# Values and gates of layer 1: another order of buffers, tables formed at the beginning, one projection moved

## The chip, the cores and the metric

The kernel runs on one core of one Trainium2 chip. The metric is the device time of one execution in microseconds. Three runs of the kernel before took 3581.37 to 3582.74 us, their median is 3581.59 us. A core has five engines with instruction streams of their own, each executed in order: TensorE (PE, with its weight loads as PEld), VectorE (DVE), ScalarE (ACT), GpSimd (POOL) and SyncE (SP, which here only issues DMAs). DMAs are issued from SP, ACT and POOL and run on 16 DMA engines.

## The reference

The reference is a two-layer backbone on 2048 latent tokens (32 rows of 64) and 256 context tokens, width 1024, in float32. Layer 0 (attention and gated linear attention) is not touched. Layer 1 is this:

```
h, hc  = modulated rms_norm of x and of the context
q, k, v, z = split(h @ w_in, 4)                 # w_in: 1024 x 4096; 16 heads of 64
q, k   = rms_norm per head
s_lat  = q . k (window of 8 rows x 16 columns) * scale + bias[head]
s_ctx  = q . k_ctx * scale
p      = softmax(concat(s_lat, s_ctx))
o      = p @ v
x      = x + gate * ((o * silu(z)) @ w_out)
```

## The kernel before

Tokens are worked on in 18 tiles of 128: tiles 0 and 1 are the context, 2 to 17 the latent tokens. `w_in` of layer 1 is cut into eight column blocks of 512, `j` = 0 to 7: 0 and 1 are the queries, 2 and 3 the keys, 4 and 5 the values, 6 and 7 the gates `z`. A matrix product in float32 precision is made of three passes: each operand is split into a high part and a rest, and `hi*hi`, `lo*hi` and `hi*lo` are summed (L129 to L131 for one tile, L190 to L192 for a pair of tiles). One projection of one tile and one block, called a cell (t, j) here, is 24 matmuls of 512 columns; a cell of gates serves a pair of tiles and is 96 matmuls of 256 columns.

Layer 1 has three stages. `odd_qk` projects queries and keys, tile by tile, and ends with the gates' block 6 of tiles 16 and 17 and the values' block 4 of these two tiles. Its work buffers come from a pool `osA`: the gains, two squares, small sums, four `onat` (a projected tile on its way to memory), two each of `oqh` and `oql` (transposed keys and queries), and four `okt` of 8 KB per partition, the keys in another order of columns. Values go to memory by POOL's DMAs (`store_v`, L1420, two for each tile), gates by POOL's (`store_z`, L1425), keys by SP's (`K1`) and POOL's (`K1t`, L1386).

`odd_vz`, the stage of the change, does two things in one interleaved stream:

- the remaining projections of values and gates (`cell`): tiles 17 and 16 first, then pairs of tiles downward. Each pair of tiles needs its modulated rows again: `reload(1, t)` loads them as `x` from the scratch tensor H (SP, L376), ACT makes the high part `hhi`, DVE the rest `hlo` (L380), in two slots that alternate with the tile number. A slot is free after the last cell of the tile that holds it. Gates are formed by ACT (tanh) and DVE (L1407), values copied by ACT, all into `ovz`, of which there are three.
- for each of 16 heads and 2048 queries, the maximum of the scores (`maxes`), which the third stage needs to form the softmax. For each head a table of biases (`mtab`, 128 x 1798, two buffers) is loaded by SP (L1476), and POOL adds two masks to it (L1477, L1478); keys `mk` (L1474) are loaded for two heads at a time and queries `mq` (L1465) for 512 at a time; ACT puts the queries into a buffer `mz` in which the other head's half is zeroed (DVE memsets, L1459); TensorE forms scores of 128 queries against the context (L1492) and against their window (L1499) in six PSUM banks `mx`, DVE reduces them (L1494) and adds the bias and reduces in one instruction (L1505).

`weave` draws from both generators: 0.57 steps of the maxima for each step of the projections (a step is three matmuls of 512 columns, or six of 256), and a projection step is held behind the maximum that lies 15 steps back.

`odd_attention`, the third stage, is not touched.

What sets the order of the instructions: the program is written with tiles in pools; when it is built, a planner with a cost estimate plays the program through and fixes, for each engine, the order in which instructions are issued: the oldest in program order among those that are ready by its estimate. On the chip each engine then keeps this order and waits, whatever has become ready behind. `issue_after(i)` adds a pure ordering: what is traced inside is placed behind `i` on its engine. Buffers of a pool lie one behind another in the order in which their names are first used; a pool that is opened where an earlier one was closed lies in the same place, and a buffer there waits for the last use of each old buffer that it overlaps. So `osB` and `omB`, the pools of `odd_vz`, lie where `osA` was.

Of the kernel before, what the change touches and what calls it, by code (L numbers as in the profile page):

```python
# [10 lines left out]
F32 = mybir.dt.float32  # L11
F32R = mybir.dt.float32r
AF = mybir.ActivationFunctionType
ALU = mybir.AluOpType
# [3 lines left out]
P = 128  # L18
D = 1024
# [4 lines left out]
NT = T // P  # L24
# [64 lines left out]
class Kern:  # L89
# [279 lines left out]
        nc.scalar.dma_start(self.H[l, t], x[:])  # L369
        return hi, lo  # L370

    def reload(self, l, t):

        nc, sp = self.nc, self.prp
        x = self.tl(sp, [P, D], "x", bufs=1)
        nc.sync.dma_start(x[:], self.H[l, t])  # L376
        h = x[:].rearrange("p (k t) -> p k t", k=KD)
        hi, lo = self.slots(t)
        self.act(hi, h)
        nc.vector.tensor_tensor(out=lo, in0=h, in1=hi, op=ALU.subtract)  # L380
        return hi, lo
# [902 lines left out]
    def odd_qk(self, ws, win, hT):  # L1284
        nc = self.nc
# [6 lines left out]
        with ExitStack() as es:  # L1292
            sp = self.pool(es, "osA", bufs=2, side="left", reuse_waits="tile")
# [98 lines left out]
            done = lambda j: j in nxt and self.od_ahead(win, ws, nxt[j])  # L1392
            cells = self.cells(list(range(NT)), (2, 3, 0, 1), lambda t, j: j > 1 or t >= NCT)[:-8]
            for j in (0, 1, 2, 3, 6, 4):
                cells += [((NT - 2, NT - 1), j)] if j == 6 else [(t, j) for t in (NT - 2, NT - 1)]
# [31 lines left out]
    def odd_vz(self, ws, win, hT):  # L1427
        nc = self.nc
        self.M1 = self.scr("M1", (16, SEQ), F32)
        NR, NC = (len(b) for b in BLOCKS["q"])  # L1430
        with ExitStack() as es:
            sp = self.pool(es, "osB", bufs=2, side="left", reuse_waits="tile")
            mp = self.pool(es, "omB", bufs=2, side="left", reuse_waits="tile")
            pp = self.pool(es, "opB", bufs=2, space=PSUM, reuse_waits="tile")
            mk = self.tl(mp, [P, NR + NC], "maskq", bufs=1)
            nc.sync.dma_start(mk[:], self.i["maskq"])

            def cell(t, j):
                wh, wl = win[j]
                w = lambda k: wh[:, k, :], lambda k: wl[k][:]  # L1440
                if j > 5:
                    for b in (0, 2):
                        ps = self.tl(pp, [P, 512], "gm")
                        yield from self.pair_steps(ps, b, w)
                        n = self.tl(sp, [P, 512], "ovz", bufs=3)
                        self.gate(n, ps[:])
                        self.store_z(t, (j - 6) * 4 + b, n)
                    return
                hi, lo = hT[t]
                ps = self.tl(pp, [P, 512], "gm")  # L1450
                yield from self.mm3_steps(ps[:], (lambda k: hi[:, k, :], lambda k: lo[:, k, :]), w, range(KD))
                n = self.tl(sp, [P, 512], "ovz", bufs=3)
                self.act(n[:], ps[:])
                self.store_v(t, j - 4, n)

            zq = [[self.tl(mp, [P, 512], f"mz{i}{a}", F32R, bufs=1) for a in range(2)] for i in range(2)]
            for i in range(2):
                for z in zq[i]:
                    nc.vector.memset(z[64 - i * 64 : 128 - i * 64].bitcast(F32), 0.0)  # L1459

            def queries(n, eng):
                h, g = divmod(n, 4)
                b = (h % 2) * 64
                q = self.tl(mp, [P, 512], "mq", F32R, bufs=1)
                eng.dma_start(q[b : b + 64].bitcast(F32), self.Q1[0, h // 2, b : b + 64, g * 512 : g * 512 + 512])  # L1465
                return q

            def maxes():
                post, q = None, queries(0, nc.sync)
                for h in range(16):  # L1470
                    j, b = h // 2, (h % 2) * 64
                    if b == 0:
                        k = self.tl(mp, [P, T], "mk", F32R, bufs=2)
                        nc.sync.dma_start(k[:].bitcast(F32), self.K1[j])  # L1474
                    tb = self.tl(mp, [P, NR, NC], "mtab", bufs=2)
                    nc.sync.dma_start(tb[:], self.i["rpb_q"][h].rearrange("p (r c) -> p r c", r=NR))  # L1476
                    nc.gpsimd.tensor_tensor(out=tb[:], in0=tb[:], in1=mk[:, :NR].unsqueeze(2).to_broadcast([P, NR, NC]), op=ALU.add)  # L1477
                    nc.gpsimd.tensor_tensor(out=tb[:], in0=tb[:], in1=mk[:, NR:].unsqueeze(1).to_broadcast([P, NR, NC]), op=ALU.add)  # L1478
                    m = self.tl(mp, [P, 16, 5], "mm")
                    nc.vector.memset(m[:], -3e38)  # L1480
                    kl = k[:, CTX:].rearrange("d (r c) -> d r c", r=32)
                    for R in range(16):
                        g, c = divmod(R, 4)
                        if c == 0:
                            zt = zq[h % 2][g % 2]
# [6 lines left out]
                        nc.tensor.matmul(pc[:, c % 2, :], lh, k[:, :CTX], start=True, stop=True)  # L1492
                        if c % 2 == 1:
                            nc.vector.tensor_reduce(out=m[:, R - 1 : R + 1, 0], in_=pc[:], axis=AX.X, op=ALU.max)  # L1494
                        (r0, nr), (c0, w) = rect("q", g, c)
                        ps = self.tl(pp, [P, 512], "mx", bufs=6)
                        a, n, d = even(c0, w)
                        ps = ps[:, : nr * n].rearrange("p (r c) -> p r c", r=nr)
                        mm = nc.tensor.matmul(ps, lh, kl[:, r0 : r0 + nr, a : a + n], start=True, stop=True)  # L1499
                        ps = ps[:, :, d : d + w]  # L1500
                        n = 1
                        for ro, ri, rn in pieces("q", 0, g, r0, nr):
                            for co, ci, cn in pieces("q", 1, c, c0, w):
                                s = ps[:, ro : ro + rn, co : co + cn]
                                nc.vector.tensor_tensor_reduce(out=s, in0=s, in1=tb[:, ri : ri + rn, ci : ci + cn], scale=1.0,  # L1505
                                                               scalar=-3e38, op0=ALU.add, op1=ALU.max, accum_out=m[:, R, n : n + 1])
                                n += 1
                        if R == 4 and post:
                            post()
                        yield mm  # L1510
                    mc = self.tl(mp, [P, 16], "mc", bufs=1)
                    nc.vector.tensor_reduce(out=mc[:], in_=m[:], axis=AX.X, op=ALU.max)

                    def post(h=h, mc=mc):
                        pt = self.tl(pp, [P, 512], "mx", bufs=6)
                        nc.tensor.transpose(pt[:16, :P], mc[:], self.ident[:])
# [422 lines left out]
```

## Time and profile before

| what | value |
|---|---|
| median of three runs | 3581.59 us |
| the profiled execution | 3587.56 us |
| its span, first to last instruction | 3585.8 us |
| mean granted clock of TensorE in it | 0.988 |

`odd_vz` begins at about 2572 us of the span and its last projections end at about 3011 us. In the profile's rows a time stands in front (us from the span's start), then the duration, the engine, the line of the kernel, the operation, and `out<-in` by the program's names; in brackets the idle time of the engine just before and what ended it. `x2` behind a row means that two like instructions are merged. In a table of stretches, the busy time of each engine stands with the number of its instructions, then the granted clock of TensorE, the busy share of the DMA engines and their GB/s. In a list of waits stand the waiting engine, line and tile, what it waited for, and then us in total, times, and the longest. Where a DMA's time to landing is given, it is from issue until its semaphore came, as minimum, median and maximum.

### The profile page before, as it was taken

The numbers are of one execution on the slowest core, as the hardware profiler recorded it, in microseconds if no ns is written. First come the engines' busy times: TensorE is split into PE (matmuls) and PEld (weight loads), VectorE is DVE, ScalarE is ACT, GpSimd is POOL, SyncE is SP. The second block draws the span as 40 slices with busy tenths as digits, with TensorE's granted clock in tenths as the row PEclk, the third lists the DMA queues.
The fourth block names the chain that finished last, engine by engine and source line by source line (L and its number), as shares of the span: only waits on it lengthen the run. The fifth ranks groups of instructions, "written<-read, shape, count | busy, mean of one in ns | idle before, by whom it ended". The sixth has DMA issues, their size and how long they took to land.

```text
span 3585.8 us, 53487 instructions
## 1 busy us (share of the span) xinstructions
PE 3499.2 (98%) x19260; PEld 2764.4 (77%) x19260; DVE 2380.5 (66%) x5020; ACT 1404.5 (39%) x2656; POOL 1221.8 (34%) x1364
## 2 busy tenths in 40 slices
PE   8999999999999999999999999999999999999899
PEld 6888998999996666656666878888798987555577
DVE  4677766888886777788765345454688783776721
ACT  5445551101116555555553034444422223555510
POOL 1433430100101222211321233333445544777743
PEclk9999999999999999999999999999999999999999
DMA  7555563222243243334543553555744338877654
GB/s 255 147 148 167 145 177 115 87 69 84 77 115 93 71 118 84 92 89 112 163 118 129 162 169 122 144 159 165 235 151 142 129 126 221 215 208 214 188 179 147
DMA packets 386834, 513.75 MB, mean 143 GB/s; under 512 B 61229, under 2 KB 263933, under 8 KB 380666
## 3 DMA queue, kind: packets, MB, share of 16 engines
q1 hardware_dynamic: 353242, 418.68, 40.8%
q0 software_dynamic: 21952, 62.74, 5.9%
q10 hardware_dynamic: 11376, 28.91, 2.3%
q8 instruction: 153, 2.51, 0.3%
q14 instruction: 111, 0.91, 0.1%
HBM read 330.61 MB, written 179.59 MB: 142 GB/s over the span
## 4 chain that ended last, share of the span: by engine, by line
PE 86%; DVE 4%; DMA 4%; ACT 2%; issue 2%; POOL 2%; SPq 0%; POOLq 0%; DVEq 0%; ACTq 0%
PE gm L131 8%; PE gm L129 8%; PE gm L130 8%; PE av L1000 7%; PE st L1058 4%; PE mx L699 4%; PE st L1060 3%; PE st L1059 3%; PE gm L190 2%; PE gm L191 2%; PE gm L192 2%; PE o L1634 2%; PE st L1604 2%; PE st L129 2%; PE st L131 2%; PE st L130 2%
## 5 line engine op out<-in xcount | busy, mean ns | idle before, releaser
L1049 DVE TENSOR_TENSOR acc<-acc,apt 128x512 f32<-128x512 f32 x512 | 379.8, 774 | 139.8 <-ACT apt L106 137.2
L700 DVE TENSOR_REDUCE mm<-mx 128x1 f32<-128x512 f32 (+1 forms) x656 | 390.6, 629 | 82.8 <-PE mx L699 75.8
L106 ACT ACTIVATE apt<-st 128x512 f32<-128x512 f32 (+1 forms) x592 | 345.7, 594 | 237.2 <-PE st L1060 197.8
L1000 PE MATMUL av<-apt,av 128*64 128x512 f32 (+1 forms) x1184 | 270.0, 592 | 0.0
L1058 PE MATMUL st<-aq,akh 97*128 97x512 f32 x576 | 244.8, 425 | 0.3 <-ACT apt L106 0.2
L699 PE MATMUL mx<-mk,mq 96*128 96x512 f32 (+1 forms) x656 | 242.9, 372 | 0.0
L106 ACT ACTIVATE u<-gm 128x352 f32<-128x352 f32 (+1 forms) x144 | 70.5, 497 | 435.1 <-PE gm L131 212.2
L1059 PE MATMUL st<-aq,akh 96*128 96x512 f32 x576 | 228.2, 396 | 0.0
L1060 PE MATMUL st<-aq,akl 96*128 96x512 f32 x576 | 228.0, 396 | 0.0
L106 ACT ACTIVATE opt<-opt 128x930 f32<-128x930 f32 (+9 forms) x144 | 119.4, 830 | 230.0 <-POOL opt L1805 137.2
L1505 DVE CUSTOM_DVE_ANT_1 mx<-mx,mtab 128x465 f32<-128x465 f32 (+12 forms) x576 | 180.1, 342 | 28.6 <-PE mx L1499 23.0
L1000 PEld LDWEIGHTS av<-apt,av 128*64 128x64 f32 x1184 | 80.1, 136 | 152.7 <-issue 150.1
L1765 DVE TENSOR_TENSOR opt<-st,tab 128x64 f32<-128x64 f32 (+10 forms) x576 | 143.0, 315 | 74.4 <-PE st L1605 41.1
L1640 POOL TENSOR_TENSOR oacc<-oacc,opt 128x682 f32<-128x682 f32 (+9 forms) x144 | 173.9, 1228 | 32.4 <-ACT opt L106 31.2
L1058 PEld LDWEIGHTS st<-aq,akh 97*128 97x128 f32 x576 | 108.3, 188 | 70.2 <-issue 42.1
L1060 PEld LDWEIGHTS st<-aq,akl 96*128 96x128 f32 x576 | 109.5, 190 | 25.2
L699 PEld LDWEIGHTS mx<-mk,mq 96*128 96x128 f32 x656 | 123.9, 189 | 6.1
L1059 PEld LDWEIGHTS st<-aq,akh 96*128 96x128 f32 x576 | 109.9, 191 | 17.3
L106 ACT ACTIVATE x<-px,modB,modA 128x128 f32<-128x128 f32 x272 | 99.3, 468 | 58.3 <-PE px L355 48.3
L131 PE MATMUL gm<-w0h,hlo 128*128 128x512 f32 x288 | 115.1, 400 | 5.0 <-DVE hlo L380 4.9
L1604 PE MATMUL st<-q,kt 128*128 128x480 f32 (+5 forms) x256 | 98.8, 388 | 20.0 <-DVE opt L1765 15.2
L129 PE MATMUL gm<-w0h,hhi 128*128 128x512 f32 x288 | 115.8, 402 | 2.3 <-DVE hhi L367 2.3
(594 smaller groups left out, 10296.5 us busy)
## 6 DMA issues: line engine op xcount, KB each, us to landing
q<-Q SPq DMA_DIRECT2D x48, 512.0 KB
H<-x ACTq DMA_DIRECT2D x36, 512.0 KB
adaw<-ada_w SPq DMA_DIRECT2D x64, 256.0 KB
x<-H SPq DMA_DIRECT2D x32, 512.0 KB
K1t<-okt POOLq DMA_DIRECT2D x32, 512.0 KB, 6.8
kt<-K1t SPq DMA_DIRECT2D x32, 512.0 KB
mtab<-rpb_q SPq DMA_DIRECT2D x16, 899.0 KB
QT<-qkhl SPq DMA_DIRECT2D x36, 384.0 KB
```

What stands on the lines that cost most here:

```text
L106: return self.nc.scalar.activation(out, in_, func, **kw)
L129: self.nc.tensor.matmul(out, lh(k), rh(k), start=j == 0, stop=False)
L130: self.nc.tensor.matmul(out, lh(k), rl(k), start=False, stop=False)
L131: yield self.nc.tensor.matmul(out, ll(k), rh(k), start=False, stop=j == n - 1)
L699: mm = nc.tensor.matmul(ps[:, :w], q[:A_QK, (t % 6) * P : (t % 6) * P + P], k[:A_QK, k0 : k0 + w], start=True, stop=True)
L700: nc.vector.tensor_reduce(out=m[:, t, n : n + 1], in_=ps[:, :w], axis=AX.X, op=ALU.max)
L1000: nc.tensor.matmul(O[j, nb][i * 64 : i * 64 + 64, :w], V[j, kt // TT][:, kt % TT, i * 64 : i * 64 + 64], pts[i][:, :w], start=n == 0, stop ...
L1049: self.add = nc.vector.tensor_tensor(out=acc[i][:, :w], in0=a[:, :w], in1=pts[i][:, :w], op=ALU.add)
L1058: nc.tensor.matmul(ps[:, :w], kh[: A_QK + 1, i, kq], qh[: A_QK + 1, :w], start=True, stop=False)
L1059: nc.tensor.matmul(ps[:, :w], kh[:A_QK, i, kq], ql[:A_QK, :w], start=False, stop=False)
L1060: mm = nc.tensor.matmul(ps[:, :w], kl[:A_QK, i, kq], qh[:A_QK, :w], start=False, stop=True)
L1505: nc.vector.tensor_tensor_reduce(out=s, in0=s, in1=tb[:, ri : ri + rn, ci : ci + cn], scale=1.0, scalar=-3e38, op0=ALU.add, op1=ALU.max, a ...
```

## The change

- `odd_qk` no longer projects block 4 of tile 16; `odd_vz` does, behind block 5 of tile 16.
- `reload` is split: `fetch_x` loads the rows; for tile 15 (`NT - 3`) it is called at the beginning of `odd_vz`.
- The two pools become one, and its buffers are first used in another order: the query, the zeroed query buffer for even heads, three `ovz`, the other three zeroed buffers, the mask, two tables, then keys and the rest.
- The bias tables of heads 0 and 1 are loaded and masked before the stream begins, ahead in program order of the first queries and keys; the other 14 are formed as before.
- The first two gate stores are placed, on POOL, behind the last of these four additions.

```
-            for j in (0, 1, 2, 3, 6, 4): ... [(t, j) for t in (NT - 2, NT - 1)]
+            ... [(t, j) for t in (NT - 2, NT - 1) if j != 4 or t == NT - 1]
...
+    def fetch_x(self, l, t):
+        x = self.tl(self.prp, [P, D], "x", bufs=1)
+        self.nc.sync.dma_start(x[:], self.H[l, t])
+        return x
...
-            sp = self.pool(es, "osB", bufs=2, side="left", reuse_waits="tile")
-            mp = self.pool(es, "omB", bufs=2, side="left", reuse_waits="tile")
+            sp = mp = self.pool(es, "omB", bufs=2, side="left", reuse_waits="tile")
             pp = self.pool(es, "opB", bufs=2, space=PSUM, reuse_waits="tile")
+            begun = {NT - 3: self.fetch_x(1, NT - 3)}
+            query = lambda: self.tl(mp, [P, 512], "mq", F32R, bufs=1)
+            zero = lambda i, a: self.tl(mp, [P, 512], f"mz{i}{a}", F32R, bufs=1)
+            wide = lambda: self.tl(sp, [P, 512], "ovz", bufs=3)
+            first = [query()]
+            zq = {(0, 0): zero(0, 0)}
+            free = [wide()]
+            for i in ((1, 0), (0, 1), (1, 1)):
+                zq[i] = zero(*i)
             mk = self.tl(mp, [P, NR + NC], "maskq", bufs=1)
             nc.sync.dma_start(mk[:], self.i["maskq"])
+            def table(h):
+                tb = self.tl(mp, [P, NR, NC], "mtab", bufs=2)
+                nc.sync.dma_start(tb[:], self.i["rpb_q"][h]...)
+                nc.gpsimd.tensor_tensor(out=tb[:], in0=tb[:], in1=mk[:, :NR]..., op=ALU.add)
+                self.added = nc.gpsimd.tensor_tensor(out=tb[:], in0=tb[:], in1=mk[:, NR:]..., op=ALU.add)
+                return tb
+            tabs = [table(h) for h in range(2)]
+            held = [self.added] * 2
...
-                        n = self.tl(sp, [P, 512], "ovz", bufs=3)
+                        n = free.pop() if free else wide()
                         self.gate(n, ps[:])
-                        self.store_z(t, (j - 6) * 4 + b, n)
+                        with self.tc.issue_after(held.pop().ins) if held else ExitStack():
+                            self.store_z(t, (j - 6) * 4 + b, n)
...
-                    tb = self.tl(mp, [P, NR, NC], "mtab", bufs=2)      # and the load and both additions
+                    tb = tabs.pop(0) if tabs else table(h)
...
-            cells = [((NT - 1, NT - 2), 7), (NT - 1, 5), (NT - 2, 5)]
+            cells = [((NT - 1, NT - 2), 7), (NT - 1, 5), (NT - 2, 5), (NT - 2, 4)]
...
-            gemms = self.stream(cells, hT, cell, lambda t: self.reload(1, t))
+            gemms = self.stream(cells, hT, cell, lambda t: self.reload(1, t, begun.pop(t, None)))
```

More of the change, by code (lines that the diff above doesn't have):

```diff
@@ L370, in modulate, with reload @@
         return hi, lo
[L372 to L376, printed above, removed]
+    def fetch_x(self, l, t):
+        x = self.tl(self.prp, [P, D], "x", bufs=1)
+        self.nc.sync.dma_start(x[:], self.H[l, t])
+        return x
+    def reload(self, l, t, x=None):
+        nc = self.nc
+        x = x or self.fetch_x(l, t)
         h = x[:].rearrange("p (k t) -> p k t", k=KD)
@@ L1394, in odd_qk @@
             for j in (0, 1, 2, 3, 6, 4):
-                cells += [((NT - 2, NT - 1), j)] if j == 6 else [(t, j) for t in (NT - 2, NT - 1)]
+                cells += [((NT - 2, NT - 1), j)] if j == 6 else [(t, j) for t in (NT - 2, NT - 1) if j != 4 or t == NT - 1]
             for _ in self.stream(cells, hT, cell, lambda t: self.prep(1, t, self.x1, pp, ("px", 2)), done):
@@ L1431, in odd_vz @@
         with ExitStack() as es:
-            sp = self.pool(es, "osB", bufs=2, side="left", reuse_waits="tile")
-            mp = self.pool(es, "omB", bufs=2, side="left", reuse_waits="tile")
+            sp = mp = self.pool(es, "omB", bufs=2, side="left", reuse_waits="tile")
             pp = self.pool(es, "opB", bufs=2, space=PSUM, reuse_waits="tile")
+            begun = {NT - 3: self.fetch_x(1, NT - 3)}
[7 more added lines that the diff above has]
+                zq[i] = zero(*i)
             mk = self.tl(mp, [P, NR + NC], "maskq", bufs=1)
             nc.sync.dma_start(mk[:], self.i["maskq"])
+            def table(h):
+                tb = self.tl(mp, [P, NR, NC], "mtab", bufs=2)
+                nc.sync.dma_start(tb[:], self.i["rpb_q"][h].rearrange("p (r c) -> p r c", r=NR))
+                nc.gpsimd.tensor_tensor(out=tb[:], in0=tb[:], in1=mk[:, :NR].unsqueeze(2).to_broadcast([P, NR, NC]), op=ALU.add)
+                self.added = nc.gpsimd.tensor_tensor(out=tb[:], in0=tb[:], in1=mk[:, NR:].unsqueeze(1).to_broadcast([P, NR, NC]), op=ALU.add)
+                return tb
+            tabs = [table(h) for h in range(2)]
+            held = [self.added] * 2
             def cell(t, j):
@@ L1451, in cell @@
                 yield from self.mm3_steps(ps[:], (lambda k: hi[:, k, :], lambda k: lo[:, k, :]), w, range(KD))
-                n = self.tl(sp, [P, 512], "ovz", bufs=3)
+                n = free.pop() if free else wide()
                 self.act(n[:], ps[:])
                 self.store_v(t, j - 4, n)
[L1456 to L1459, printed above, removed]
+            for (i, _), z in zq.items():
+                nc.vector.memset(z[64 - i * 64 : 128 - i * 64].bitcast(F32), 0.0)
             def queries(n, eng):
@@ L1463, in queries @@
                 b = (h % 2) * 64
-                q = self.tl(mp, [P, 512], "mq", F32R, bufs=1)
+                q = first.pop() if first else query()
                 eng.dma_start(q[b : b + 64].bitcast(F32), self.Q1[0, h // 2, b : b + 64, g * 512 : g * 512 + 512])
@@ L1474, in maxes @@
                         nc.sync.dma_start(k[:].bitcast(F32), self.K1[j])
-                    tb = self.tl(mp, [P, NR, NC], "mtab", bufs=2)
-                    nc.sync.dma_start(tb[:], self.i["rpb_q"][h].rearrange("p (r c) -> p r c", r=NR))
-                    nc.gpsimd.tensor_tensor(out=tb[:], in0=tb[:], in1=mk[:, :NR].unsqueeze(2).to_broadcast([P, NR, NC]), op=ALU.add)
-                    nc.gpsimd.tensor_tensor(out=tb[:], in0=tb[:], in1=mk[:, NR:].unsqueeze(1).to_broadcast([P, NR, NC]), op=ALU.add)
+                    tb = tabs.pop(0) if tabs else table(h)
                     m = self.tl(mp, [P, 16, 5], "mm")
@@ L1484, in maxes @@
                         if c == 0:
-                            zt = zq[h % 2][g % 2]
+                            zt = zq[h % 2, g % 2]
                             self.by_tile(zt[b : b + 64], q[b : b + 64])
```

## The prediction

> **What bounds the kernel now.** I read the page first, then the waits of TensorE around the edit, then stretches and rows of that place.
>
> ```profile
> span 3585.8 us, 53487 instructions
> ...
> PE 3499.2 (98%) x19260; PEld 2764.4 (77%) x19260; DVE 2380.5 (66%) x5020; ACT 1404.5 (39%) x2656; POOL 1221.8 (34%) x1364
> ```
>
> TensorE is the bound: 3499.2 of 3585.8 us, and the change leaves its matmuls as many as before. A gain can only be TensorE time that is lost now. The waits of TensorE from 2540 to 3030, which hold the whole stage of values and gates:
>
> ```profile
> PE gm L131 <- DVE hlo L380: 4.9, 1, 4.9
> PE gm L129 <- DVE ovz L1407: 2.1, 1, 2.1
> PE mx L1492 <- DMA mk<-K: 0.8, 1, 0.8
> ```
>
> The other two entries are 0.6 and 0.5 us. All three stand at the stage's beginning. Stretches there (busy time of PE, PEld, DVE, ACT, POOL, then the granted clock, DMA share, GB/s), and TensorE's own rows:
>
> ```profile
> 2555.00:2560.00 5.00, 5.00 (x23) 4.10 (x22) 4.62 (x8) 3.38 (x7) 3.21 (x5) 1.00 1.00 289
> 2560.00:2565.00 5.00, 5.00 (x23) 4.13 (x22) 0.27 (x1) 0.35 (x1) 1.09 (x2) 1.00 0.98 302
> 2576.10:2578.20 2.10, 0.04 (x2) 0.03 (x1) 0.69 (x1) 1.71 (x3) 0.00 (x0) 1.00 0.97 407
> 2578.20:2582.80 4.60, 3.75 (x12) 3.20 (x13) 1.89 (x3) 0.00 (x0) 1.35 (x2) 0.64 0.96 356
> 2593.90:2598.80 4.90, 0.06 (x1) 0.00 (x0) 4.90 (x2) 0.00 (x0) 3.76 (x2) 0.77 0.29 80
> 2598.80:2603.30 4.50, 4.47 (x11) 3.51 (x12) 2.35 (x16) 1.31 (x2) 0.00 (x0) 0.50 0.30 117
> ```
>
> ```profile
> 2559.55 0.39 PE L129 MATMUL gm<-w0h,hhi 128*128 128x512 f32 x1
> 2565.04 0.28 PE L190 MATMUL gm<-hhi,w3h 128*128 128x256 f32 x1
> 2575.83 0.28 PE L192 MATMUL gm<-hhi,w3l 128*128 128x256 f32 x1
> 2578.17 0.50 PE L129 MATMUL gm<-w1h,hhi 128*128 128x512 f32 x1 [2.06 <-DVE ovz L1407]
> 2579.51 0.55 PE L1492 MATMUL mx<-mk,mz 128*128 128x256 f32 x1 [0.85 <-DMA mk<-K]
> 2599.85 0.63 PE L130 MATMUL gm<-w0l,hhi 128*128 128x512 f32 x1
> 2600.27 0.63 PE L131 MATMUL gm<-w0h,hlo 128*128 128x512 f32 x1
> 2603.56 0.39 PE L130 MATMUL gm<-w0l,hhi 128*128 128x512 f32 x1
> 2603.78 0.39 PE L131 MATMUL gm<-w0h,hlo 128*128 128x512 f32 x1
> ```
>
> After each gap the clock is down: at 0.50 one matmul follows the last after 0.42 us, later after 0.22, 0.23 in the long run (24 in 2559.55 to 2565.04).
>
> First gap: 2.06 idle, then 4.60 us with 12 matmuls, 8 short ones of the maxima (about 0.14 each at full clock) and 4 of 0.23, 2.0 us of work; 2.06 + 2.6 = 4.6 lost. Second gap: 4.9 idle, then 11 matmuls (2.5 us) in 4.5 us; 4.9 + 2.0 = 6.9. Together **11.5 us, 0.32%**, the most that this edit can win here.
>
> Who makes the gaps:
>
> ```profile
> 2504.60 0.33 SPq L376 DMA_DIRECT2D x<-H  x1
> 2566.13 1.05 POOL L1420 DMA_DIRECT2D V<-onat  x2 [4.41 <-ACT onat L106]
> 2572.20 0.35 SPq L1436 DMA_DIRECT2D maskq<-maskq  x1
> 2572.31 1.03 DVE L1459 MEMSET mz<- 64x512 f32 x2 [12.04 <-DMA V<-onat]
> 2573.46 0.45 SPq L1474 DMA_DIRECT2D mk<-K  x1
> 2576.28 0.63 ACT L106 ACTIVATE mz<-mq 64x512 fp32r<-64x512 f32 x1 [10.44 <-DMA mq<-Q]
> 2577.43 0.69 DVE L1407 SCALAR_TENSOR_TENSOR ovz<-ovz,gm 128x512 f32<-128x512 f32 x1 [2.72 <-ACT ovz L106]
> 2582.18 3.20 POOL L1477 TENSOR_TENSOR mtab<-mtab,maskq 128x1798 f32<-128x1798 f32 x1 [3.04 <-DMA mtab<-rpb_q]
> 2588.51 10.26 DVE L380 TENSOR_TENSOR hlo<-x,hhi 128x1024 fp32r<-128x1024 f32 x1 [6.09 <-ACT hhi L106]
> 2594.01 3.67 POOL L1478 TENSOR_TENSOR mtab<-mtab,maskq 128x1798 f32<-128x1798 f32 x1
> 2603.07 1.23 DVE L380 TENSOR_TENSOR hlo<-x,hhi 128x1024 fp32r<-128x1024 f32 x1 [2.15 <-ACT hhi L106]
> ```
>
> The first: mask and zeroed queries lie where the last values (`onat`) are still being stored. SP's mask load and DVE's memset wait for that store, the query load stands behind the mask, and ACT, in order, waits 10.44 us for the query before it may read the first gate, which DVE then frees at 2578.1. The second: `hlo` of tile 15 takes 10.26 us instead of 1.23. It begins at 2588.51, amid the four table adds (2582.18 to 2597.68), and ends 1.1 us after the last.
>
> [...]
>
> **The change, part by part.** The profiled execution took 3587.56 us, 1.8 more than its span and 6.0 more than the median 3581.59; savings are counted in the former and carried to the median.
>
> *(16, 4) moves* from before the pair's gates to behind (16, 5): 24 matmuls, 5.5 us, zero net on TensorE. The pair then ends at 2576.1 − 5.5 = 2570.6, and tile 15's conversion gets 5.5 us more cover. Its two POOL stores and ACT copy move along; POOL's V stores of tile 17 move up to where tile 16's stand, 2560.6.
>
> *x of tile 15 first*: zero. It was issued at 2504.60 already, 80 us before use.
>
> *Layout*: one pool, in order query, mz00, three ovz, mz10, mz01, mz11, mask, two tables, two K. By the sizes in the code the old buffers in that space are squares, four `onat`, `oqh`, `oql`, then `okt` (4 x 8 KB). So query and mz00 fall on squares, which are long dead; mz10 and the third ovz on the `onat` that (17, 4) will take; the mask on `oqh`; tables on `oql` and `okt20/21`; K on `okt21/30`. The wait for V leaves SP and ACT, but stays on DVE with mz10's memset, with the first gate's DVE half queued behind it if the planner keeps them in that order. I take that it does: in its estimate the store was done long before the gate, as ACT's order shows (mz ahead of a gate ready 5 us sooner).
>
> *Tables*: two loads move past the query and K loads on SP, four adds (2 x 3.2 + 2 x 3.7 = 13.8 us) to the front of POOL, two gate stores (0.74 each) behind them. Landings now, by issue windows:
>
> ```profile
> L1386 POOL DMA_DIRECT2D K1t<-okt x2: 622/624/627, 2548.8 to 2549.4; - x2
> DMA to landing us min/median/max: 7.9/9.1/10.2
> L1386 POOL DMA_DIRECT2D K1t<-okt x2: 626/636/647, 2555.9 to 2556.6; - x2
> DMA to landing us min/median/max: 8.4/9.5/10.6
> L1420 POOL DMA_DIRECT2D V<-onat x2: 532/544/557, 2560.6 to 2561.2; - x2
> DMA to landing us min/median/max: 10.2/10.3/10.4
> ```
>
> `okt21` is free at 2549.4 + 10.2 = 2559.6, so both tables are on their way from there on, 1.8 MB into DMA engines that are 98 to 100% busy with stores. A table costs them 2.7 us (now K lands at 2579.5, the table behind it at 2582.2, where its add starts). I put the adds at about 2565 to 2580. Tile 15's `hlo` comes after (17, 5), not before 2577, and has (16, 5) and (16, 4), 11 us, as cover: even a full collision to 2580 is hidden. **The second gap goes: 6.9 us.** Without that cover it would cost up to 10.26 − 1.23 again.
>
> *When TensorE goes on after the pair* is the unknown, by two chains.
> - K rows: `okt30` lands at 2556.6 + 10.6 = 2567.2, the load takes 6.0 (2573.46 to 2579.5): 2573.2 at best, 2578.6 with both tables ahead of it.
> - DVE: V of tile 17 lands in the place of tile 16's, 2571.4, and up to 5.4 later with both tables let in; a memset (0.5) and the gate (0.7) follow: 2572.6 to 2578.0.
>
> That the second chain vanishes by another order is possible; then the gap could be nothing, so the lower end is zero loss. I take 2576, with one of the two tables paid in either chain: the engines have 7 us for the tables before K's load, and run full. Gap 2576 − 2570.6 = 5.4, and 2.0 for the slow clock as after the gap of 4.9: 7.4 lost instead of 4.6. The ends 2572.6 and 2578.6 give 3.3 to 10.0 lost.
>
> *Waits added*: the gate stores stand behind the last add; three ovz buffers carry to the copy of (16, 5), which waits until the first is stored, and (15, 4) waits for that copy. Stored at 2580 + 0.7 + 8.2 (longest landing below) = 2589, needed at about 2576 + 16.5 + 2 = 2594. Zero, with 5 us to spare.
>
> ```profile
> L1425 POOL DMA_DIRECT2D z<-ovz x2: 728/735/742, 2578.4 to 2585.3; - x2
> DMA to landing us min/median/max: 3.5/5.8/8.2
> ```
>
> **Sum**: 11.5 − 7.4 = 4.1 us saved; 3587.6 becomes 3583.5, and the median **3577.5** (−0.11%). The planner orders everything behind anew; I allow 1 or 2 us for it either way, in the tails up to 4. The rest of the stage loses 1.1 us on TensorE now, so little can be won there.
>
> **Rivals.**
> - *Both gaps go*: the gate precedes the memset on DVE and the first maxima fall behind (17, 5), so K is there. For it: mq and mz00 are free early. Against: rows of these stores land 10 us late, and the planner's order did not foresee it. 1 us left: 3581.6 − 10.5 = 3571.
> - *The stage starts later than now* (slower): if the mask or a table meets a buffer that V still holds, SP queues mask, tables, query and K behind it until 2572.2 as today, with two tables ahead of K: 2579.5 + 5.4 = 2585. Gap 14.4 + 2.0 = 16.4, less 11.5: 4.9 slower, 3586.5. It loses from a restart after 2570.6 + 11.5 − 2.0 = 2580.1 on. Against: the layout puts the mask on `oqh`, not `onat`.
>  [...]
> - *Gate stores hold the projections*: adds that end after 2585 let (15, 4) wait where it waits today. The second gap stays at 6.9 and the first costs 7.4: 3584.4. It speaks for it that the mask's landing gates the first add; 5 us of slack against.
>
> **How the numbers follow.** Forecast 0.52, both gaps gone 0.25, late start 0.13, gate stores 0.10. The forecast's own range is 3574 to 3580, by its ends. 0.2% (7.2 us: below 3574.4, above 3588.8) is about what a measurement of this kernel tells from no change. Faster: 0.25 and 0.04 of the forecast's tail, 0.29. Slower: half of late start and gate stores, 0.12, since re-planning can add the 2 to 4 us that they lack. Same: the rest, 0.59. For 8 in 10 the range reaches from the case of both gaps gone to the late start: 3570.5 to 3586.5.
>
> **What the new profile would show.** Right: no TensorE wait on `hlo` near 2600 and an `hlo` of about 1.2 us for tile 15; adds near 2565; the pair's last matmul 5.5 us sooner; a TensorE gap of 3 to 8 us at or after the pair, ended by K's landing or by a DVE gate behind a memset that waited for V. Wrong: no gap there (both gone); mask issued after 2570 (late start); (15, 4) waiting for an ACT copy that waits for z (gate stores); or new TensorE waits on `hlo` later in the stage, which would say that re-planning, not the start, sets the result.

## The result, and the profile after

The changed kernel is slower: 3597.61 us in the median (3595.79 to 3601.28) against 3581.78 us before (3575.27 to 3584.92) on the same chip, a ratio of 1.0055 with a 95% interval of 1.0042 to 1.0067; the medians are 15.8 us apart. The forecast was 3577.5 us with a range up to 3586.5.

The profiled execution took 3600.18 us, at a mean granted clock of 0.985. The page of after:

```profile
span 3598.3 us, 53481 instructions
...
PE 3503.1 (97%) x19260; PEld 2766.5 (77%) x19260; DVE 2379.1 (66%) x5020; ACT 1403.4 (39%) x2656; POOL 1218.9 (34%) x1364
```

TensorE works 4 us longer than before, on as many matmuls, and the span is 12.5 us longer: TensorE waits more. To find where, I took from both traces the time at which the n-th matmul begins. As many matmuls stand in each, and a cell that moves a little does not matter between marks that lie before and behind it. Differences to before, in us:

| stretch (matmul count; time before) | after |
|---|---|
| up to 13200 (2550.9): stages in which nothing is changed | −4.6 |
| 13200 to 13600 (2626.9): the beginning of the stage of values and gates | −2.5 |
| 13600 to 16000 (2995.8): the rest of it | −1.6 |
| 16000 to 16200 (3036.0): the beginning of `odd_attention` | **+18.9** |
| 16200 to the end | +2.3 |
| sum | +12.5 |

The first row says how far two single executions differ without any cause: 4.6 us. The edited stage saves 4.1 us, as much as the prediction's sum had. The loss is in the stage behind it, whose code is not touched.

The stage's beginning. TensorE's waits from 2540 to 2625 in after have one entry over 0.5 us:

```profile
PE gm L129 <- DVE ovz L1412: 6.9, 1, 6.9
```

and the rows of that place (start, duration, engine and line, as before):

```profile
2570.33 0.48 DVE L1481 MEMSET mz<- 64x512 f32 x1 [14.09 <-DMA V<-onat]
...
2572.21 1.21 DVE L1412 SCALAR_TENSOR_TENSOR ovz<-ovz,gm 128x512 f32<-128x512 f32 x2
2581.82 2.75 DVE L385 TENSOR_TENSOR hlo<-x,hhi 128x1024 fp32r<-128x1024 f32 x1 [8.39 <-ACT hhi L106]
...
2556.01 1.09 POOL L1425 DMA_DIRECT2D V<-onat  x2 [1.52 <-ACT onat L106]
2569.79 6.36 POOL L1454 TENSOR_TENSOR mtab<-mtab,maskq 128x1798 f32<-128x1798 f32 x2 [12.69 <-issue]
2576.11 7.37 POOL L1455 TENSOR_TENSOR mtab<-mtab,maskq 128x1798 f32<-128x1798 f32 x2
...
2558.09 0.35 SPq L1449 DMA_DIRECT2D maskq<-maskq  x1
2558.61 3.48 SPq L1453 DMA_DIRECT2D mtab<-rpb_q  x2
...
2563.86 2.68 SPq L1496 DMA_DIRECT2D mk<-K  x2
```

That is the forecast's picture: mask, tables and keys are loaded early, the additions come first, `hlo` is short and nobody waits for it, and DVE's memset waits for the store of the last values (V) with the first gate queued behind it.

The beginning of `odd_attention`. Waits of TensorE from 2990 to 3050, its first matmul there, and stretches, in after:

```profile
PE st L1623 <- DMA q<-Q: 8.4, 1, 8.4
```

```profile
3009.30 1.62 PE L1623 MATMUL st<-q,kc 128*128 128x512 f32 x3 [8.36 <-DMA q<-Q]
```

```profile
3000.00:3010.00 10.00, 1.64 (x7) 1.07 (x6) 0.00 (x0) 0.60 (x1) 0.00 (x0) 0.72 0.71 173
3010.00:3020.00 10.00, 8.86 (x23) 6.12 (x22) 5.24 (x4) 4.35 (x8) 4.27 (x2) 0.50 1.07 299
3020.00:3030.00 10.00, 8.38 (x23) 4.88 (x23) 6.99 (x26) 4.23 (x7) 5.61 (x4) 0.50 1.10 261
```

The same 20 us before:

```profile
3010.00:3020.00 10.00, 9.47 (x41) 5.26 (x41) 6.95 (x28) 7.26 (x13) 3.10 (x3) 1.00 0.95 235
3020.00:3030.00 10.00, 10.00 (x68) 6.45 (x66) 4.53 (x10) 4.64 (x8) 5.42 (x5) 1.00 1.04 273
```

TensorE stands 8.36 us for a load of `q`, and then runs for more than 20 us at a granted clock of 0.50, with 46 matmuls on record where before there are 109. Over the 200 matmuls from 16000 to 16200 it is idle for 11.4 us against 0.8 before (8.4 of them this wait) and busy for 47.8 us against 39.5: of the 18.9 us, 10.6 are waiting, and 8.3 are more busy time on the same matmuls.

Why is `q` late? SP's issues in after, with ScalarE's stores of the context tiles' values (V1c):

```profile
2970.99 0.32 SPq L375 DMA_DIRECT2D x<-H  x1
2971.40 1.77 SPq L111 DMA_DIRECT2D q<-Q  x3
...
2987.19 6.77 SPq L111 DMA_DIRECT2D kc<-K1t  x2
2998.11 6.61 SPq L111 DMA_DIRECT2D q<-Q  x3
...
2985.13 0.32 ACTq L1421 DMA_DIRECT2D V1c<-ovz  x1
2990.62 0.33 ACTq L1421 DMA_DIRECT2D V1c<-ovz  x1
2996.11 0.33 ACTq L1421 DMA_DIRECT2D V1c<-ovz  x1
3001.61 0.33 ACTq L1421 DMA_DIRECT2D V1c<-ovz  x1
```

and SP's before:

```profile
2967.05 1.80 SPq L111 DMA_DIRECT2D q<-Q  x3
...
2979.71 0.34 SPq L376 DMA_DIRECT2D x<-H  x1
2980.40 1.04 SPq L111 DMA_DIRECT2D kc<-K1t  x2
2981.50 1.87 SPq L111 DMA_DIRECT2D q<-Q  x3
```

In the list of SP's waits from 2600 to 3080 the entry for these stores grows. Before:

```profile
SPq L111 <- DMA V1c<-ovz: 4.0, 2, 3.3
```

After:

```profile
SPq L111 <- DMA V1c<-ovz: 26.5, 4, 11.5
```

The loads of `kc` and `q` do not read what these stores write, and their buffers do not overlap `ovz` (by the buffers' addresses in the two programs). What they share is the semaphore that tells a transfer's end. In the trace SP's and ScalarE's transfers take eight of them (100, 101, 103, 104, 106 to 109) in turn, in planned order, and none of the 1319 transfers on them was issued before the one ahead of it on its semaphore had landed. For after:

```
issued   transfer      semaphore
2985.13  ACT V1c<-ovz  100
2987.19  SP  kc<-K1t   100
2990.62  ACT V1c<-ovz  101
2993.34  SP  kc<-K1t   101
2996.11  ACT V1c<-ovz  103
2998.11  SP  q<-Q      103
3001.61  ACT V1c<-ovz  104
3003.64  SP  q<-Q      104
```

The four stores land at 2987.11, 2993.32, 2998.10 and 3003.63, each at most 0.1 us ahead of the load behind it. The load of 3003.64 lands at 3009.16, and TensorE begins at 3009.30.

So the four stores stand ahead of `kc` and the second `q` in the plan of after, and behind them in the plan of before. Theory A: this comes from the merging of the pools. `ovz` is used until the last projection; in one pool with tables, keys and queries, it keeps the whole pool's memory, in the planner's account, from the next stage until then, and the loads into that memory are planned later. Rival B: the new places of the buffers. Rival C: the moved projection, or the tables loaded first.

### The profile page after: what moved, and what is told of

Read it like the earlier page. It is cut to its first block, busy times and chain, and to the rows that moved or that the text cites. A ratio compares the mean times of both kernels' runs of the same rounds, so it can differ in the third digit from the quotient of the medians.

```text
span 3598.3 us, 53481 instructions
## 1 busy us (share of the span) xinstructions
PE 3503.1 (97%) x19260; PEld 2766.5 (77%) x19260; DVE 2379.1 (66%) x5020; ACT 1403.4 (39%) x2656; POOL 1218.9 (34%) x1364
## 4 chain that ended last, share of the span: by engine, by line
PE 82%; DMA 7%; DVE 4%; POOL 2%; issue 2%; ACT 2%; SPq 0%; POOLq 0%; DVEq 0%; ACTq 0%
PE gm L129 8%; PE gm L131 8%; PE gm L130 8%; PE av L1005 7%; PE st L1063 4%; PE mx L704 4%; PE st L1065 4%; PE st L1064 4%; PE gm L190 2%; PE gm L191 2%; PE gm L192 2%; PE o L1653 2%; PE st L1623 2%; PE o L1635 2%; PE pj L129 2%
## 5 line engine op out<-in xcount | busy, mean ns | idle before, releaser
L1524 DVE CUSTOM_DVE_ANT_1 mx<-mx,mtab 128x217 f32<-128x217 f32 (+11 forms) x576 | 179.8, 342 | 30.5 <-PE mx L1518 25.1
L129 PE MATMUL gm<-w1h,hhi 128*128 128x512 f32 x288 | 116.0, 403 | 6.9 <-DVE ovz L1412 6.9
```

What stands on the lines that cost most here:

```text
L129: self.nc.tensor.matmul(out, lh(k), rh(k), start=j == 0, stop=False)
```

## The experiments

Times are medians; `before` was run on the same chip beside each. The table at the end has all of them by stretch.

**One pool cut in three, every buffer at the changed kernel's address.**

```
-            sp = mp = self.pool(es, "omB", bufs=2, side="left", reuse_waits="tile")
+            op = self.pool(es, "oqB", bufs=2, side="left", reuse_waits="tile")
+            sp = self.pool(es, "osB", bufs=2, side="left", reuse_waits="tile")
+            mp = self.pool(es, "omB", bufs=2, side="left", reuse_waits="tile")
...
-            query = lambda: self.tl(mp, [P, 512], "mq", F32R, bufs=1)
-            zero = lambda i, a: self.tl(mp, [P, 512], f"mz{i}{a}", F32R, bufs=1)
+            query = lambda: self.tl(op, [P, 512], "mq", F32R, bufs=1)
+            zero = lambda i, a: self.tl(mp if i or a else op, [P, 512], f"mz{i}{a}", F32R, bufs=1)
```

> The changed kernel with its one pool cut in three (query rows and first query buffer; ovz; all the rest), every buffer kept at the address that the changed kernel gives it. Theory A (the merged pool: ovz now keeps the tables', keys' and queries' memory from being handed to the next stage, so that stage's first loads are planned behind the four V1c stores, and wait on the chip for these stores to land): the stall of TensorE on q<-Q at L1623, 8.4 us in the changed kernel, and the granted clock of 0.50 behind it are gone, the gain of 4 us at the stage's start stays, and the time is 3576 to 3582 us, 15 to 20 us under the changed kernel. Rival B (the new addresses delay the loads) and rival C (the moved projection or the tables loaded first): the addresses, the cells and the tables are those of the changed kernel, so the stall stays at 6 to 9 us and the time at 3595 to 3600.

Measured: 3580.13 against 3583.67 us, ratio 0.9990 (0.9981 to 0.9999). The stall is gone; no single wait of TensorE at that place is over 0.7 us, and SP's issues show why:

```profile
2964.22 1.05 SPq L111 DMA_DIRECT2D kc<-K1t  x2
2965.32 1.87 SPq L111 DMA_DIRECT2D q<-Q  x3
...
2969.11 0.33 SPq L375 DMA_DIRECT2D x<-H  x1
```

`kc` and the second `q` are issued at 2964 to 2967, 16 us and more before the first V1c store (2983.24), and at addresses that are those of after. The beginning of `odd_attention` costs +0.4 us instead of +18.9. B and C fall as causes of the loss, as far as one trial can say.

**The kernel before with its two pools merged, and nothing else.**

```
-            sp = self.pool(es, "osB", bufs=2, side="left", reuse_waits="tile")
-            mp = self.pool(es, "omB", bufs=2, side="left", reuse_waits="tile")
+            sp = mp = self.pool(es, "omB", bufs=2, side="left", reuse_waits="tile")
...
+            wide = lambda: self.tl(sp, [P, 512], "ovz", bufs=3)
+            free = [wide()]
...
-                n = self.tl(sp, [P, 512], "ovz", bufs=3)
+                n = free.pop() if free else wide()
```

`free` is filled first so that `ovz` keeps its place in front.

> The kernel before with nothing changed but that osB and omB are one pool, ovz first, so that every buffer has its old address. Theory A: the start of the next stage loses what the changed kernel lost, 15 to 20 us: TensorE waits 6 to 10 us for q<-Q at L1623 (L1604 of before), SP's queue waits some 25 us for V1c's stores, and the time is 3596 to 3602, with no gain at the stage's start. Rival B (addresses) and rival C (moved projection, tables first): 3580 to 3584, as before.

Measured: 3602.73 against 3583.67 us, ratio 1.0053 (1.0040 to 1.0065): this one line alone makes the whole loss. TensorE's wait, and SP's issues:

```profile
PE st L1605 <- DMA q<-Q: 8.3, 1, 8.3
```

```profile
2970.14 0.32 SPq L376 DMA_DIRECT2D x<-H  x1
2970.56 1.78 SPq L111 DMA_DIRECT2D q<-Q  x3
...
2986.33 6.57 SPq L111 DMA_DIRECT2D kc<-K1t  x2
2997.26 6.66 SPq L111 DMA_DIRECT2D q<-Q  x3
```

They are those of after, one by one. One part of the expectation missed: I wrote that there is no gain at the stage's beginning, and there is one of 5.3 us. The `hlo` of tile 15 took 5.38 us here against 10.26, and TensorE did not wait for it:

```profile
2583.92 5.38 DVE L380 TENSOR_TENSOR hlo<-x,hhi 128x1024 fp32r<-128x1024 f32 x1 [6.33 <-ACT hhi L106]
...
2584.48 3.72 POOL L1479 TENSOR_TENSOR mtab<-mtab,maskq 128x1798 f32<-128x1798 f32 x1
```

`hlo` ended 1.1 us after this addition, the third of four, while the fourth began at 2589.25; in before it ended 1.1 us after the last one. So some us of shift between two engines seem to decide whether the second gap is there; no trial varies that shift alone.

**The kernel before with the projection moved alone.**

```
-  [(t, j) for t in (NT - 2, NT - 1)]
+  [(t, j) for t in (NT - 2, NT - 1) if j != 4 or t == NT - 1]
...
-  cells = [((NT - 1, NT - 2), 7), (NT - 1, 5), (NT - 2, 5)]
+  cells = [((NT - 1, NT - 2), 7), (NT - 1, 5), (NT - 2, 5), (NT - 2, 4)]
```

> The kernel before with the one value projection of tile 16 moved into the stage, and nothing else: its pools, addresses and table loads are the old ones. Theory A: no stall at the next stage's start; the time within 4 us of before, 3578 to 3586. Rival C (the moved projection shifts the planned order of the stores against the loads): a stall of some us on q<-Q and 3590 to 3600.

Measured: 3583.32 against 3583.67 us, ratio 1.0000 (0.9992 to 1.0009); no stall behind. Rival C falls for the projection. At the stage's beginning it wins nothing: the pair's gates come 6 us earlier, and the first of them waits 8.93 us (2.06 before) for the same store:

```profile
2578.17 1.03 DVE L1459 MEMSET mz<- 64x512 f32 x2 [16.30 <-DMA V<-onat]
...
2581.17 0.79 PE L129 MATMUL gm<-w1h,hhi 128*128 128x512 f32 x1 [8.93 <-DVE ovz L1407]
```

**Two pools, `ovz` in front as before; all else as in the changed kernel.**

```
-            sp = mp = self.pool(es, "omB", bufs=2, side="left", reuse_waits="tile")
+            sp = self.pool(es, "osB", bufs=2, side="left", reuse_waits="tile")
+            mp = self.pool(es, "omB", bufs=2, side="left", reuse_waits="tile")
```

> The changed kernel with two pools, ovz's first and the rest behind it, so ovz lies at its old address and the zeroed queries do not; every other line as in the changed kernel. Theory A: two pools are enough, no stall on q<-Q, 3576 to 3584; beside the version with three pools it tells what the new places of the buffers alone are worth at the stage's start: the gate of the first pair or the memsets may wait for other buffers of the earlier stage, by up to 5 us. Rival C: the stall stays and 3592 to 3600. Rival B (addresses): as C or as A, by whether ovz's or the tables' new place was the cause.

Measured: 3579.37 against 3583.67 us, ratio 0.9990 (0.9982 to 0.9999), no stall. The order of buffers is worth nothing by itself: the gate's gap is 7.5 us here and 7.1 with three pools. Both versions load the tables first, without the loss, so rival C falls for the tables too.

**The changed kernel with the V1c stores on GpSimd's queue.**

```
-            self.nc.scalar.dma_start(self.V1c[f, :, t, :], v[:])
+            self.nc.gpsimd.dma_start(self.V1c[f, :, t, :], v[:])
```

> The changed kernel, its one pool and its planned order of loads kept, with the four stores of V1c (and the one of the other value half) for the two context tiles issued by GpSimd instead of ScalarE. Theory A says that the loads of q and kc wait for V1c only because SP's and ScalarE's transfers take the same eight semaphores in turn: with the stores on GpSimd's queue SP waits no more than 5 us for V1c, TensorE's stall on q<-Q falls from 8.4 to 0 to 2 us, and the time is 3578 to 3586. The rival: the loads are late because of the order itself (the third x row's load ahead of them) or because they wait for memory: then the stall stays at 6 to 9 us and the time at 3594 to 3601.

Measured: 3587.89 against 3581.39 us, ratio 1.0021 (1.0011 to 1.0030). SP's order of loads is that of after, no entry for V1c is left among SP's waits, and `kc` goes out right behind the first `q`:

```profile
2975.34 0.32 SPq L375 DMA_DIRECT2D x<-H  x1
2975.75 1.79 SPq L111 DMA_DIRECT2D q<-Q  x3
...
2978.38 1.35 SPq L111 DMA_DIRECT2D kc<-K1t  x2
2979.79 2.96 SPq L111 DMA_DIRECT2D q<-Q  x3
```

The stall on `q` is gone, as theory A has it; but the beginning of `odd_attention` still costs 6.9 us. So the shared semaphores carry 12 of the 18.9 us (one execution of each), and the median stands 2 us above the range that I gave. The rest had to be the later place of the loads or the stores on GpSimd.

**The same stores on GpSimd, with three pools.** (The edits of the first trial and of the last one together.)

> The version with three pools at the changed kernel's addresses, with V1c's stores on GpSimd as well. With one pool and these stores on GpSimd the start of the last stage still lost 5 us of the 17. If the place of q's loads behind the third x row's load costs these 5 us, they are gone here, where q comes first: within 3 us of the version with three pools, 3577 to 3583. If the stores on GpSimd's queue cost them, they stay: 3583 to 3588.

Measured: 3582.29 against 3581.52 us, ratio 1.0001 (0.9988 to 1.0013); the beginning of `odd_attention` costs +0.4 us. With the loads planned early, GpSimd's queue costs nothing there; so the 6.9 us go with the later place of the loads in the plan. By which waits they come about is not taken apart: 3.4 us are more idle time of TensorE and 3.4 more busy time.

**Is it the last use of `ovz`?** Two trials gave the last four values of the stage, those of the context tiles, one buffer in a pool of their own, with the merged pool left as it is.

```
+            cp = self.pool(es, "ocB", bufs=2, side="left", reuse_waits="tile")
...
-                n = free.pop() if free else wide()
+                n = self.tl(cp, [P, 512], "ovc", bufs=1) if t < NCT else free.pop() if free else wide()
```

In the first trial the new pool lies behind `omB`, in the second in front of it.

> The changed kernel with its one pool and its addresses, where only the four values of the context tiles, the last projections of the stage, go to one buffer in a pool of their own behind the old one. If the last use of ovz is what keeps the merged pool's memory from the next stage's plan, that last use is now four projections (22 us) earlier: the stall on q<-Q falls from 8.4 to under 2 us and most of the loss goes, 3578 to 3586. If merging costs in another way, the stall stays: 3594 to 3601.

Measured: 3597.85 against 3581.52 us, ratio 1.0054 (1.0037 to 1.0071), TensorE's wait 12.0 us. This says nothing on the question, since the new buffer lay on memory that `kc` takes, so that its load (3001.55) waited for all four stores by right.

> The trial with a buffer of its own for the four context values, repeated with that buffer in front of the merged pool: behind the pool it lay on memory that the last stage's first context keys take, so that their load had to wait for the last of these stores, which said nothing on the question. Everything else of the changed kernel lies 2 KB further. If the last use of ovz keeps the merged pool's memory from the next stage's plan, q's and kc's loads now come ahead of the last V1c stores: the stall on q<-Q under 2 us, the loss at the last stage's start under 7 us of the 17, 3578 to 3587. If merging costs in another way, the stall stays and 3594 to 3601.

Measured: 3591.03 against 3580.77 us, ratio 1.0032 (1.0019 to 1.0044), above what I expected. SP and ScalarE:

```profile
2974.77 1.77 SPq L111 DMA_DIRECT2D q<-Q  x3
...
2977.08 1.04 SPq L111 DMA_DIRECT2D kc<-K1t  x2
2978.75 5.12 SPq L111 DMA_DIRECT2D q<-Q  x3
...
2988.49 0.32 ACTq L1421 DMA_DIRECT2D V1c<-ovc  x1
2996.17 0.60 ACT L106 ACTIVATE ovc<-gm 128x512 f32<-128x512 f32 x1 [7.71 <-DMA V1c<-ovc]
```

The loads have moved: `kc` and the second `q` are issued ahead of the first V1c store, 10 us or more earlier than in after, and TensorE does not wait for `q` any more. Moving the last use of `ovz` out of the pool moves the next stage's loads, so by this trial the pool's last use is what counts. What the trial gained it gave back in part: with one buffer each copy waits for the store before it to land (7.71 us in the row), and TensorE waited 6.5 us for the last copy. The beginning of `odd_attention` costs 8.8 us.

**Without the loss: what is the rest of the change worth?** Two pools, the projection left in the earlier stage:

```
-            sp = mp = self.pool(es, "omB", bufs=2, side="left", reuse_waits="tile")
+            sp = self.pool(es, "osB", bufs=2, side="left", reuse_waits="tile")
+            mp = self.pool(es, "omB", bufs=2, side="left", reuse_waits="tile")
...
-                ... [(t, j) for t in (NT - 2, NT - 1) if j != 4 or t == NT - 1]
+                ... [(t, j) for t in (NT - 2, NT - 1)]
...
-            cells = [((NT - 1, NT - 2), 7), (NT - 1, 5), (NT - 2, 5), (NT - 2, 4)]
+            cells = [((NT - 1, NT - 2), 7), (NT - 1, 5), (NT - 2, 5)]
```

> The changed kernel with two pools (ovz's own) and the value projection of tile 16 left in the earlier stage. The split versions lose 7.1 and 7.5 us on the first pair's gate against 2.1 before, and the kernel before with the projection moved alone loses 8.9: if that is the price of the moved projection (the pair comes 6 us earlier, the memsets wait for the last store of V<-onat all the same), the gate's gap is 1 to 3 us here and TensorE's second gap (4.9 us on hlo before) stays under 1.5, since the tables' additions still come early: 3574 to 3580. If the gate's gap comes from the order of buffers, it stays at 6 to 8 us and the time at 3578 to 3582.

Measured: 3575.75 against 3581.39 us, ratio 0.9986 (0.9975 to 0.9996). The gate's gap is 3.0 us, the gap on `hlo` is gone, the stage's beginning saves 6.0 us where the same kernel with the projection moved saved 2.4. By stretch, moving it cost 3.6 us; these are single executions, and the intervals of the two kernels (0.9982 to 0.9999 and 0.9975 to 0.9996) overlap.

Three pools and other places, so that what the first gate stands behind lies on memory that is free early (`mz00` and `mz01` on the old squares, `ovz`, mask, the first table, `mz10` and `mz11` on `oqh`, `oql` and the first two `okt`); only the second `mk` lies on `onat`. With the projection moved, and not moved:

```
...
+            zq = {i: zero(*i) for i in ((0, 0), (0, 1))}
+            keep("mk1")
+            free = [wide()]
+            mk = self.tl(mp, [P, NR + NC], "maskq", bufs=1)
+            for n in ("mm", "mtab0"):
+                keep(n)
+            for i in ((1, 0), (1, 1)):
+                zq[i] = zero(*i)
+            keep("mtab1")
+            first = [query()]
+            keep("mk0")
...
```

`keep` takes a buffer at this point and hands it out at its first use; `mtab` and `mk` become two names each with one buffer. `mz00`, `mz01` and `mk1` are in one pool, `ovz` in the second, the rest in the third.

> The changed kernel with three pools and other places: the first gate's buffer, the four zeroed query buffers and the first table lie on memory of the earlier stage that is free early, and only the second key buffer lies on onat. If the memsets behind V<-onat's store are what the first gate waits for, the gap on ovz falls from 7 us to under 1.5, and with the stall of the next stage gone too the time is 3570 to 3577. If the gate waits for something else, the gap stays at 5 us or more: 3578 to 3582.

> As the version with three pools and other places, with the value projection of tile 16 left in the earlier stage. If the gate's buffers are free early anyhow, the projection's place is worth nothing: within 2 us of that version, 3570 to 3578. If the projection is needed to cover the additions of the tables, the gap on hlo or on ovz comes back with 2 to 5 us: 3575 to 3582.

Measured: 3575.15 (ratio 0.9983, 0.9974 to 0.9991) and 3572.49 us (0.9977, 0.9968 to 0.9986), against 3581.39. Memsets and first gate of the second:

```profile
2559.34 2.20 DVE L1495 MEMSET mz<- 64x512 f32 x4
...
2570.28 0.69 DVE L1412 SCALAR_TENSOR_TENSOR ovz<-ovz,gm 128x512 f32<-128x512 f32 x1 [8.57 <-ACT ovz L106]
```

and its stretches over the old two gaps:

```profile
2570.00:2580.00 10.00, 10.00 (x68) 9.10 (x67) 1.38 (x2) 1.36 (x3) 3.99 (x3) 1.00 0.95 348
2580.00:2590.00 10.00, 10.00 (x51) 8.49 (x50) 7.37 (x28) 3.87 (x5) 10.00 (x6) 1.00 0.34 101
```

The memsets are done 8.7 us before the gate's DVE half; TensorE is busy from 2570 to 2590 without a gap, at full clock. The beginning saves 12.0 us; the prediction put the most that can be won there at 11.5. This version is faster than both kernels, by 0.23% than the one before. Whether the 2.7 us between the two versions come from the projection's place is not settled by their intervals; by stretch it is 3.3 us at the stage's beginning.

All by stretch of the matmul count, difference to before in us (one execution each; the first column is chance):

| kernel | to 13200 | to 13600 | to 16000 | to 16200 | to the last matmul |
|---|---|---|---|---|---|
| the change | −4.6 | −2.5 | −1.6 | +18.9 | +2.3 |
| three pools | −5.0 | −2.5 | −3.1 | +0.4 | +2.6 |
| before, pools merged | −4.1 | −5.3 | −0.2 | +18.0 | +0.7 |
| before, projection moved | +1.6 | +0.1 | −0.7 | +0.4 | −0.6 |
| two pools | −0.6 | −2.4 | −3.1 | +0.4 | −2.7 |
| change, stores on GpSimd | +1.8 | −3.0 | −3.1 | +6.9 | +1.1 |
| three pools, stores on GpSimd | −4.3 | −1.7 | −3.1 | +0.4 | +4.0 |
| change, own context buffer, behind | −5.3 | −2.7 | −2.9 | +19.7 | −0.8 |
| change, own context buffer, in front | −2.5 | +0.3 | −3.1 | +8.8 | 0.0 |
| two pools, projection not moved | −5.3 | −6.0 | −2.5 | +1.4 | −4.3 |
| other places, projection moved | +0.9 | −8.7 | −2.0 | +0.4 | −4.0 |
| other places, not moved | −1.1 | −12.0 | −0.6 | 0.0 | −4.9 |

## Why the prediction was wrong, point by point

- *TensorE is the bound, and only its lost time counts*: right, in both directions.
- *11.5 us is the most to be won at the beginning*: right; the version without gaps won 12.0 there.
- *(16, 4): zero net*: wrong by some 3.6 us (3.3 in the pair with other places), by single executions. Moving it lets the pair's gates come earlier than the store they stand behind, so cover turns into waiting (8.93 us alone, 6.9 in the change), as the step on TensorE's restart has it; but the prediction counted only the covering of `hlo`, not that leaving the projection in place would be better.
- *Layout*: right for the stage itself. Mask, tables and keys were early, the wait for V stayed on DVE with `mz10`'s memset, and the gate stood behind it. This answers the rivals too: it is neither "both gaps go" (the gate had a gap of 6.9), nor the late start (the mask went out at 2558.09), and no projection waited for a gate's store.
- *Restart at 2576, gap 5.4*: with this execution's 4.6 us that is 2571.4; it was 2572.89, a gap of 6.9. The chain that set it was DVE's, not the keys', which were issued at 2563.86 already. The last store of V, issued at 2556.57, landed at 2570.00, after 13.4 us where the sum had 10.4 and allowed, by my estimate of 2.7 us a table, up to 5.4 more for the tables. In the kernel with the projection moved alone, whose first table goes out only at 2568.35, the same store took 15.1 us; which transfers make it late is not shown.
- *The second gap goes*: right, with less to spare. The additions ran from 2569.79 to 2583.48, 8 to 9 us later than the forecast's 2565 to 2580 less those 4.6: the first table landed 11.0 us after its issue, at 2569.57. `hlo` of tile 15 met the last addition and took 2.75 us, not 1.2, and nobody waited.
- *Gate stores*: right, zero.
- *Sum 4.1*: the stage gave 4.1 us, 2.5 at its beginning and 1.6 behind. The nearness is partly luck, with 1.5 us more gap and some gain in the rest of the stage where I had none; what gave that gain is not traced. The lower end of the forecast's own range, with 3.3 us lost, is 3573.4 and not 3574.
- **The step that failed** is "The planner orders everything behind anew; I allow 1 or 2 us for it either way, in the tails up to 4". It was +18.9 us, at one place, and merging the pools alone, in the kernel before, cost 18.0 us there. The part on the layout had read the merged pool as a new order of addresses, and looked at which old buffers the new ones wait for; it did not look at who takes the memory behind. Before, the memory of tables, keys and queries was out of use with the last maxima, while `ovz` was needed to the last projection; the list of SP's waits and the first issues of `q`, `kc` and `tab`, 26 to 43 us ahead of the last projections' end, were in the trace of before. Their being early was a cover that I did not name, and the merge took it away. No rival had this in it either: the slower rival was put at the stage's beginning.

## What to carry to other kernels

Pools are not only places: where a planner frees memory by pool, a buffer that lives longest decides when all its neighbours can be filled again, so short-lived and long-lived buffers belong in different pools, whatever the addresses. When a change touches the end of buffers' lives, the prediction must look at the stage behind it, at the loads that are issued ahead of its first use. And a transfer that is planned late can stand behind transfers that have nothing to do with it, by the semaphores that they share: 26.5 us of SP's waits in after.

## What the runs showed of the hardware that was not expected

- SP's loads waited 26.5 us in after for stores on ScalarE's queue that have no data or memory in common with them, on semaphores of which the two queues share eight. With these stores on GpSimd's queue no such wait was left, and TensorE lost 6.9 us there instead of 18.9.
- The gap on `q` cost more than itself. Behind 8.36 us of waiting TensorE ran for over 20 us at a granted clock of 0.50 while its matmuls came sparsely (23 in 10 us), as the rows of 3010 to 3030 have it, and its busy time grew by 8.3 us. In the stage of values and gates of the same kernel, after the gap of 6.9 us, the clock was full again within 8 us:

```profile
2575.00:2580.00 5.00, 5.00 (x17) 3.96 (x17) 0.00 (x0) 0.00 (x0) 5.00 (x3) 0.72 0.26 87
2580.00:2585.00 5.00, 5.00 (x26) 4.26 (x26) 3.19 (x4) 2.06 (x3) 5.00 (x4) 1.00 0.15 38
```

- The same subtraction (`hlo`) beside GpSimd's additions took 10.26, 5.38 and 2.75 us in three kernels (before, pools merged, the change), and 1.23 us at 2603.07 in before, with no addition beside it. In each of the three it ended 1.1 us after the end of an addition (2597.68, 2588.20 and 2583.48).
